# The first group's gates in a hybrid decoder step: raw products copied into the convolution's input tile

## The chip, the cores and the metric

The kernel runs as one program on one core of a Trainium2 chip. Its time is device time in microseconds (us) for one execution; lower is better. The core has five engines, each with an instruction queue of its own that is worked off in order: PE (TensorE, matrix products), DVE (VectorE), ACT (ScalarE), POOL (GpSimd) and SP (SyncE, which here only issues transfers).

## The reference

One layer of a decoder trunk is run for a prompt of 2048 tokens and for eight sample sequences of 4 tokens each, in float32. Cut to what matters here:

```python
h = rms_norm(x, w_norm1) * (1 + sc1) + sh1
proj = h @ w_in                    # all heads' q, k, v, gates from one projection
qkv, conv_new = short_conv(dn_qkv, conv_buf, w_conv)      # width 4, then silu
...                                # DeltaNet: per 64-token chunk in the reference
tmat = lower + eye(C)
sol = triangular_solve(tmat, rhs, lower=True, unit_diagonal=True)
...
o_dn  = rms(o_dn)  * w_dn_norm  * silu(dn_z)              # gated_head_norm
o_gla = rms(o_gla) * w_gla_norm * silu(gr)
x = x + gt1 * (concat(o_dn, o_gla) @ w_o)
...                                # then an MLP with squared ReLU, and a last norm
```

There are four DeltaNet heads and four GLA heads of 128 columns each. The gates that this change touches are `silu(dn_z)` and `silu(gr)`: eight projections of 128 columns, each followed by `z / (1 + exp(-z))`.

## The kernel before

The tokens are worked in four groups. Group 0 holds the 32 sample tokens and the first 512 of the prompt (544 columns, as two blocks of 272); groups 1 to 3 hold 512 prompt tokens each, one block. Activations lie transposed, 128 features on the partitions and tokens along the free axis. A product of float32 numbers is made of three products of rounded parts (`prod`, lines 243 to 245), so one projection of 128 columns is 8 x 3 matmuls per block, 48 in group 0. It goes into one of two PSUM banks named `gps`.

In group 0 every weight block is loaded once (line 221, on SP's queue), split into a high part (ACT, line 225) and a low part (DVE, line 226), and both are stored to DRAM (line 201); later groups load the two parts (line 217). The tiles `wb` have six buffers, and one block is prepared ahead.

Within a group the source goes: the four key projections, the four query projections, the four DeltaNet gates, the four value projections, and then for each GLA head its key, query and gate. A key, query or value projection ends in `conv`: ACT copies the product from PSUM into `craw` (one buffer, lines 824 to 827), DVE makes the width-4 convolution from it (lines 834 and 836), and a sigmoid follows. A `gate` reads its product twice on ACT, for the exponential (line 458) and, in group 0 alone, for a plain copy (line 462); the sigmoid follows (lines 153 to 155), DVE multiplies (line 464), and SP stores the result to `zscr` (line 465). In groups 1 to 3 DVE multiplies straight from PSUM.

Behind the first query projection the source calls `dn_inverse`, for the unit triangular matrices of the DeltaNet. DVE solves 32 x 32 blocks by 30 steps of two instructions (lines 912 and 914); the result goes to DRAM and back, head by head, into cleared tiles `Tm` (lines 921 and 923); a vector transpose (line 927) and small matmuls with copies between them (lines 933 to 953) put the blocks together. For each of the four heads it asks for three tiles of the name `t2`: one `Tm` and two `yt`. The name `t2` has three buffers. The result `Um` is first read in `dn_chain` (line 1015), which runs over the tokens in order and stands behind the first GLA key projection in the source.

Who waits for whom is not written by hand. The tile framework takes the instructions, in the order of the source as priority, and fixes an order for each engine; a tile that finds no free buffer of its name waits until an earlier one is released. So an engine's order differs from the source's where something had to wait. `sp` is the pool of such tiles, two buffers to a name unless `bufs` says otherwise. `rb` is a small tile in `dn_decay` (lines 797 to 799): four times, for group 0 alone, DVE writes it and a matmul reads it.

Of the kernel before, what the change touches and what calls it, by code (L numbers as in the profile page):

```python
# [8 lines left out]
F32 = mybir.dt.float32  # L9
# [7 lines left out]
P = 128  # L17
# [59 lines left out]
def tile_trunk(ctx: ExitStack, tc: tile.TileContext, a: dict):  # L77
# [8 lines left out]
    def gps():  # L86
        return pp.tile([P, 512], F32, name="gps", bufs=2)

    def mps():
        return pp.tile([P, 512], F32, name="mps", bufs=3)  # L90
# [7 lines left out]
    sp = stage.enter_context(tc.tile_pool(name="sp", bufs=2))  # L98
# [22 lines left out]
    def c32(k):  # L121
        o, n = NC32[k]
        return cf[:, o:o + n]
# [27 lines left out]
    def sigm(x):  # L151

        V.tensor_scalar(out=x, in0=x, scalar1=1e18, scalar2=None, op0=MIN)
        S.activation(out=x, in_=x, func=AF.Ln, bias=1.0)
        S.activation(out=x, in_=x, func=AF.Exp, scale=-1.0)
# [75 lines left out]
    def split(name, idx, nk=8, raw=None):  # L231
        hi, lo = ahead.pop((name, idx), None) or parts(name, idx, raw)
        if plan and plan[0] == (name, idx):
            plan.pop(0)
            if plan:
                ahead[plan[0]] = parts(*plan[0])
        return hi.rearrange("p (k c) -> p k c", k=nk), lo.rearrange("p (k c) -> p k c", k=nk)

    def prod(ps, w, x, ks, xs):

        n = len(ks)
        for i, (kw, kx) in enumerate(zip(ks, xs)):
            T.matmul(ps, lhsT=w[0][:, kw], rhs=x[0](kx), start=(i == 0), stop=False)  # L243
            T.matmul(ps, lhsT=w[0][:, kw], rhs=x[1](kx), start=False, stop=False)  # L244
            T.matmul(ps, lhsT=w[1][:, kw], rhs=x[0](kx), start=False, stop=(i == n - 1))  # L245

    def proj(g, blk, h):

        w = split("w_in", blk)
        out = []  # L250
        for c0, c1 in BLK[g]:
            ps = gps()
            prod(ps[:, 0:c1 - c0], w, (lambda k: h[0][:, k, c0:c1], lambda k: h[1][:, k, c0:c1]), range(8), range(8))
            out.append((ps[:, 0:c1 - c0], c0, c1))
        return out
# [197 lines left out]

    def gate(g, ct, h, blk):

        for ps, c0, c1 in proj(g, blk, h):
            e = sp.tile([P, 512], F32, name="e", bufs=3)[:, 0:c1 - c0]
            S.activation(out=e, in_=ps, func=AF.Exp, scale=-1.0)
            z = ps
            if g == 0:  # L460
                z = sp.tile([P, 512], F32, name="t2", bufs=3)[:, 0:c1 - c0]
                S.copy(out=z, in_=ps)
            sigm(e)
            V.tensor_tensor(out=e, in0=z, in1=e, op=MUL)
            Y.dma_start(out=zscr[ct, :, GC[g] + c0:GC[g] + c1], in_=e)
# [272 lines left out]
    def dn_decay(g, d, sm, sms):  # L738
# [34 lines left out]
        if g == 0:  # L773
            gs = sp.tile([32, 4], F32, name="gs", bufs=1)
            bs = sp.tile([32, 4], F32, name="bs", bufs=1)
            dn_gates(sms.unsqueeze(1), 32, 1, gs.unsqueeze(2), bs.unsqueeze(2))
            ps = mps()
            T.matmul(ps[0:32, 0:4], lhsT=c32("tri_s")[0:32], rhs=gs, start=True, stop=True)
            T.matmul(ps[0:32, 8:12], lhsT=c32("same_s")[0:32], rhs=gs, start=True, stop=True)
            gb = sp.tile([32, 4, 8], F32, name="gbs", bufs=1)  # L780
            V.tensor_tensor(out=gb, in0=gs.unsqueeze(2).broadcast_to([32, 4, 8]),
                            in1=c32("seq_s")[0:32].unsqueeze(1).broadcast_to([32, 4, 8]), op=MUL)
            pl = mps()
            T.matmul(pl[:, 0:32], lhsT=ones[0:32], rhs=gb.rearrange("p h b -> p (h b)"), start=True, stop=True)
            eLs = sp.tile([P, 4, 8], F32, name="eLs", bufs=1)
            S.activation(out=eLs, in_=pl[:, 0:32].rearrange("p (h b) -> p h b", h=4), func=AF.Exp)
            Gs = sp.tile([32, 4], F32, name="Gs", bufs=1)
            eGs = sp.tile([32, 4], F32, name="eGs", bufs=1)
            kcs = sp.tile([32, 4], F32, name="kcs", bufs=1)
            V.tensor_copy(out=Gs, in_=ps[0:32, 0:4])  # L790
            S.activation(out=eGs, in_=Gs, func=AF.Exp)
            V.tensor_tensor(out=kcs, in0=ps[0:32, 8:12], in1=Gs, op=SUB)
            S.activation(out=kcs, in_=kcs, func=AF.Exp)

            pb = mps()
            for hd in range(4):
                rb = sp.tile([P, P], F32, name="rb")
                V.tensor_scalar(out=rb[0:32], in0=ones[0:32], scalar1=gs[:, hd:hd + 1], scalar2=None, op0=MUL)
                T.matmul(pb[:, hd * 32:hd * 32 + 32], lhsT=rb[0:32], rhs=c32("tri_s")[0:32], start=True, stop=True)
            eGb = sp.tile([P, 4, 32], F32, name="eGbs", bufs=1)  # L800
            S.activation(out=eGb, in_=pb[:, 0:128].rearrange("p (h t) -> p h t", h=4), func=AF.Exp)
            Da = sp.tile([32, 4, 32], F32, name="Das", bufs=1)
            Db = sp.tile([32, 4, 32], F32, name="Dbs", bufs=1)
            for hd in range(4):
                for dst, mk in ((Da, "mas"), (Db, "mbs")):
                    V.scalar_tensor_tensor(out=dst[:, hd], in0=pb[0:32, hd * 32:hd * 32 + 32], scalar=Gs[:, hd:hd + 1],
                                           in1=c32(mk)[0:32], op0=SUB, op1=ADD)
            S.activation(out=Da, in_=Da, func=AF.Exp)
            S.activation(out=Db, in_=Db, func=AF.Exp, scale=-1.0)
            d.update(bs=bs, eGs=eGs, kcs=kcs, eLs=eLs, eGb=eGb, Da=Da, Db=Db)  # L810
            d["qv"] = sp.tile([P, 4, 3, 32], F32, name="qvs", bufs=1)
# [4 lines left out]
    def conv(g, ct, blocks, dst):  # L816

        off, tg = OFF[g], TG[g]
        raw = sp.tile([P, 515], F32, name="craw", bufs=1)
        xs = None  # L820
        for ps, c0, c1 in blocks:
            if c0 < off:
                xs = sp.tile([P, 8, 7], F32, name="xs")
                S.copy(out=xs[:, :, 3:7], in_=ps[:, 0:32].rearrange("p (b t) -> p b t", t=4))
                S.copy(out=raw[:, 3:3 + c1 - off], in_=ps[:, off:c1])  # L825
            else:
                S.copy(out=raw[:, 3 + c0 - off:3 + c1 - off], in_=ps)
        if g == 0:
            V.memset(raw[:, 0:3], 0.0)
        else:  # L830
            V.tensor_copy(out=raw[:, 0:3], in_=halo[0][:, ct, :])
        V.tensor_copy(out=halo[1][:, ct, :], in_=raw[:, 512:515])
        cp = dst[:, off:tg]
        V.tensor_scalar(out=cp, in0=raw[:, 0:512], scalar1=wconv[:, ct, 0:1], scalar2=None, op0=MUL)
        for i in range(1, 4):
            V.scalar_tensor_tensor(out=cp, in0=raw[:, i:i + 512], scalar=wconv[:, ct, i:i + 1], in1=cp, op0=MUL, op1=ADD)  # L836
        if g == 0:
            V.tensor_copy(out=xs[:, :, 0:3], in_=cst[:, ct])
            V.tensor_copy(out=cso[:, ct], in_=xs[:, :, 4:7])
            c4 = dst[:, 0:32].rearrange("p (b t) -> p b t", t=4)  # L840
            V.tensor_scalar(out=c4, in0=xs[:, :, 0:4], scalar1=wconv[:, ct, 0:1], scalar2=None, op0=MUL)
            for i in range(1, 4):
                V.scalar_tensor_tensor(out=c4, in0=xs[:, :, i:i + 4], scalar=wconv[:, ct, i:i + 1], in1=c4, op0=MUL, op1=ADD)
        e = sp.tile([P, 544], F32, name="ce", bufs=1)
        S.activation(out=e[:, 0:tg], in_=dst[:, 0:tg], func=AF.Exp, scale=-1.0)
        sigm(e[:, 0:tg])
        V.tensor_tensor(out=dst[:, 0:tg], in0=dst[:, 0:tg], in1=e[:, 0:tg], op=MUL)
# [19 lines left out]
    def dn_kproj(g, hd, h, d):  # L867
        conv(g, 4 + hd, proj(g, 12 + (hd // 2) * 8 + hd % 2, h), d["kT"][:, hd])
# [86 lines left out]
    def dn_qproj(g, hd, h, d):  # L955
        d["qT", hd] = sp.tile([P, 544], F32, name="cv")
        conv(g, hd, proj(g, 12 + (hd // 2) * 8 + 2 + hd % 2, h), d["qT", hd])
# [25 lines left out]
    def dn_vproj(g, hd, h, d):  # L983
        d["vT", hd] = sp.tile([P, 544], F32, name="cv")
        conv(g, 8 + hd, proj(g, 12 + (hd // 2) * 8 + 4 + hd % 2, h), d["vT", hd])
# [145 lines left out]
    def group(g):  # L1131
# [18 lines left out]
        def decays():  # L1150
            dn_decay(g, d, ts[0][1], ts[0][3])
# [46 lines left out]
        for hd in range(4):  # L1198
            step(lambda: gate(g, hd, h, 12 + (hd // 2) * 8 + 6 + hd % 2))
# [31 lines left out]
    sp = ctx.enter_context(tc.tile_pool(name="sp2", bufs=2))  # L1231
# [215 lines left out]
```

## Time and profile before

| what | value |
|---|---|
| time, median of 3 runs | 2951.27 us (2944.88 to 2957.69) |
| the profiled execution | 2961.44 us, span of the profile 2959.6 us |
| PE busy | 2835.0 us, 96% of the span |
| PE weight loads busy | 2400.3 us, 81% |
| DVE busy | 1494.0 us, 50% |
| ACT busy | 889.6 us, 30% |
| POOL busy | 265.9 us, 9% |
| mean granted clock of PE | 0.979 of full |

The span runs from the first to the last instruction of the profile; the profiled execution took 1.8 us more than its span and is one execution, which lies 10.2 us above the median of the three timed ones. Matmuls are pipelined, so a busy PE is not a PE at its peak. Idle time of an engine counts only where another engine waits for it.

### The profile page before, as it was taken

To read this page: it belongs to the slowest core of one execution; us is meant where nothing else is said; L and a number is where in the kernel's file an instruction comes from. 1 tells how busy PE (TensorE), PEld (TensorE's weight loads), DVE (VectorE), ACT (ScalarE), POOL (GpSimd) and SP (SyncE) were. 2 spreads that over 40 slices of the span, in tenths; PEclk is the share of its full clock that TensorE was granted. 3 is DMA by queue.
4 is the path that set the end of the run, shared out by engine and by line. 5 is a ranking of instruction groups with operands and counts; after the bars stand their busy time and mean duration, and the time that the engine had idled before them with its cause. 6 is when DMAs were issued, how large, how long until landed. Compare 5 with 4: busy or idle time off the path is not lost.

```text
span 2959.6 us, 43982 instructions
## 1 busy us (share of the span) xinstructions
PE 2835.0 (96%) x17311; PEld 2400.3 (81%) x17311; DVE 1494.0 (50%) x3564; ACT 889.6 (30%) x2238; POOL 265.9 (9%) x204
## 2 busy tenths in 40 slices
PE   7949999999999999989999999999899999999997
PEld 5849987887778777778899999999778888888886
DVE  5957778766767677547333333333744222222225
ACT  3625544344434344324122211222222100011102
POOL 0100000000000000041211212112210000000000
PEclk9969999999999999999999999999999999999999
DMA  7525644456536554586433333334774222222224
GB/s 274 193 73 197 230 149 156 141 168 243 196 124 216 178 175 147 197 281 235 152 144 128 143 136 131 146 129 148 273 259 160 100 99 87 100 93 92 100 88 154
DMA packets 174271, 476.08 MB, mean 161 GB/s; under 512 B 36960, under 2 KB 50656, under 8 KB 173296
## 3 DMA queue, kind: packets, MB, share of 16 engines
q1 hardware_dynamic: 167520, 451.88, 44.0%
q0 software_dynamic: 6544, 21.38, 2.3%
q8 instruction: 137, 2.24, 0.3%
q14 instruction: 70, 0.57, 0.1%
HBM read 331.68 MB, written 141.79 MB: 160 GB/s over the span
## 4 chain that ended last, share of the span: by engine, by line
PE 80%; DVE 8%; DMA 5%; issue 3%; ACT 2%; SPq 1%; POOL 1%; DVEq 0%; POOLq 0%; ACTq 0%
PE gps L244 12%; PE gps L245 12%; PE gps L243 12%; PE cps L244 10%; PE cps L245 10%; PE cps L243 10%; PE gps L419 1%; PE mps L419 1%; DMA wb<-w_in 1%; DMA zo<-zscr 1%; PE mps L1019 1%; DVE cv L836 1%; DVE Um L914 1%; PE mps L629 1%; DVE tb L912 1%
## 5 line engine op out<-in xcount | busy, mean ns | idle before, releaser
L243 PE MATMUL gps<-hb,wb 128*128 128x512 f32 (+1 forms) x1752 | 631.8, 361 | 5.0 <-ACT craw L825 3.0
L245 PE MATMUL gps<-hb,wb 128*128 128x512 f32 (+1 forms) x1752 | 625.7, 357 | 1.8 <-DMA wb<-k_w_o 1.6
L244 PE MATMUL gps<-hb,wb 128*128 128x512 f32 (+1 forms) x1752 | 627.2, 358 | 0.0
L243 PEld LDWEIGHTS gps<-hb,wb 128*128 128x128 f32 x1752 | 333.1, 190 | 57.5 <-issue 7.1
L244 PEld LDWEIGHTS gps<-hb,wb 128*128 128x128 f32 x1752 | 332.9, 190 | 44.4 <-issue 2.7
L245 PEld LDWEIGHTS gps<-hb,wb 128*128 128x128 f32 x1752 | 332.5, 190 | 44.5 <-DMA wb<-k_w_o 2.5
L245 PE MATMUL cps<-hb,wb 128*128 128x512 f32 (+1 forms) x968 | 343.9, 355 | 5.4 <-POOL wb L226 5.4
L243 PE MATMUL cps<-hb,wb 128*128 128x512 f32 (+1 forms) x968 | 343.4, 355 | 5.0 <-DVE gas L1247 3.7
L244 PE MATMUL cps<-hb,wb 128*128 128x512 f32 (+1 forms) x968 | 343.9, 355 | 0.0
L226 POOL TENSOR_TENSOR wb<-wb 128x1024 fp32r<-128x1024 f32 x72 | 172.4, 2394 | 746.4 <-PE gps L244 412.7
L243 PEld LDWEIGHTS cps<-hb,wb 128*128 128x128 f32 x968 | 183.7, 190 | 32.5 <-issue 4.1
L245 PEld LDWEIGHTS cps<-hb,wb 128*128 128x128 f32 x968 | 183.8, 190 | 32.0 <-POOL wb L226 6.1
L244 PEld LDWEIGHTS cps<-hb,wb 128*128 128x128 f32 x968 | 183.6, 190 | 26.5 <-issue 0.2
L225 ACT CAST wb<-wb 128x1024 fp32r<-128x1024 f32 (+1 forms) x104 | 109.2, 1050 | 307.5 <-DMA wb<-w_up 160.5
L1295 ACT ACTIVATE e<-cps 128x512 f32<-128x512 f32 (+1 forms) x96 | 50.0, 520 | 498.2 <-PE cps L245 498.1
L1298 DVE CAST a<-e 128x272 fp32r<-128x272 f32 (+1 forms) x96 | 58.7, 613 | 251.8 <-ACT e L1296 251.8
L1298 DVE CAST x<-e 128x512 fp32r<-128x512 f32 x64 | 27.3, 427 | 277.6 <-ACT e L1296 277.6
L243 PE MATMUL cps<-a,wb 128*128 128x272 f32 (+1 forms) x460 | 149.8, 326 | 5.8 <-DVE gas L1247 4.4
L244 PE MATMUL cps<-a,wb 128*128 128x272 f32 (+1 forms) x460 | 149.4, 325 | 0.0
L245 PE MATMUL cps<-a,wb 128*128 128x272 f32 (+1 forms) x460 | 149.0, 324 | 0.0
L1295 ACT ACTIVATE e<-gps 128x512 f32<-128x512 f32 (+1 forms) x64 | 32.8, 513 | 341.2 <-PE gps L245 340.1
L1243 DVE SCALAR_TENSOR_TENSOR a<-cps,modT,a 128x512 f32<-128x512 f32 (+1 forms) x81 | 58.1, 718 | 134.2 <-PE cps L245 134.2
(472 smaller groups left out, 5213.4 us busy)
## 6 DMA issues: line engine op xcount, KB each, us to landing
wb<-k_w_in SPq DMA_DIRECT2D x168, 512.0 KB, 4.3
wb<-k_w_up SPq DMA_DIRECT2D x80, 512.0 KB, 4.2
wb<-k_w_down SPq DMA_DIRECT2D x80, 512.0 KB, 4.2
k_w_up<-wb SPq DMA_DIRECT2D x64, 512.0 KB, 2.8
k_w_down<-wb SPq DMA_DIRECT2D x64, 512.0 KB, 2.8
k_w_in<-wb SPq DMA_DIRECT2D x56, 512.0 KB, 3.1
wb<-k_w_o SPq DMA_DIRECT2D x48, 512.0 KB, 4.5
wb<-w_up SPq DMA_DIRECT2D x32, 512.0 KB, 3.7
```

What stands on the lines that cost most here:

```text
L225: S.copy(out=hi, in_=raw[:, 0:n])
L226: (V if name in ("w_in", "w_ts0", "w_ts1") else G).tensor_tensor(out=lo, in0=raw[:, 0:n], in1=hi.bitcast(F32), op=SUB)
L243: T.matmul(ps, lhsT=w[0][:, kw], rhs=x[0](kx), start=(i == 0), stop=False)
L244: T.matmul(ps, lhsT=w[0][:, kw], rhs=x[1](kx), start=False, stop=False)
L245: T.matmul(ps, lhsT=w[1][:, kw], rhs=x[0](kx), start=False, stop=(i == n - 1))
L419: T.matmul(ps, lhsT=h[hh][:, 4 * q + kk, c0:c0 + P], rhs=w[:, kk, :], start=(kk == 0 and i == 0), stop=(kk == 3 and i == 2))
L629: T.matmul(pa[0:i0, n, i0:i0 + 32], lhsT=ko[:, n, o:o + I, :], rhs=Q3[:, n, i0:i0 + 32], start=True, stop=True)
L836: V.scalar_tensor_tensor(out=cp, in0=raw[:, i:i + 512], scalar=wconv[:, ct, i:i + 1], in1=cp, op0=MUL, op1=ADD)
L912: V.tensor_tensor(out=t, in0=Lb[:, j + 1:32, j:j + 1].broadcast_to([64, 31 - j, j]), in1=Tb[:, j:j + 1, 0:j].broadcast_to([64, 31 - j, j]) ...
L1243: V.scalar_tensor_tensor(out=out[:, lo:c1], in0=ps[:, lo - c0:c1 - c0], scalar=modT[:, gv, 0:1], in1=x[:, lo:c1], op0=MUL, op1=ADD)
L1295: S.activation(out=r, in_=ps, func=AF.Relu)
L1298: V.tensor_copy(out=hi, in_=r)
```

## The change

In group 0 the gate's plain copy of the product goes into a part of a `craw` tile, one tile for both blocks, and no longer into a `t2` tile for each block. The convolution asks for `craw` with 544 columns, so that both uses have one size; it still works with 515 of them. `craw` keeps one buffer. `rb` goes from two buffers to one, which frees 512 bytes on each partition; the larger `craw` takes 116 of them.

```diff
@@ gate
+        zs = sp.tile([P, 544], F32, name="craw", bufs=1) if g == 0 else None
         for ps, c0, c1 in proj(g, blk, h):
             e = sp.tile([P, 512], F32, name="e", bufs=3)[:, 0:c1 - c0]
             S.activation(out=e, in_=ps, func=AF.Exp, scale=-1.0)
             z = ps
             if g == 0:
-                z = sp.tile([P, 512], F32, name="t2", bufs=3)[:, 0:c1 - c0]
+                z = zs[:, c0:c1]
                 S.copy(out=z, in_=ps)
             sigm(e)
             V.tensor_tensor(out=e, in0=z, in1=e, op=MUL)
@@ dn_decay
-                rb = sp.tile([P, P], F32, name="rb")
+                rb = sp.tile([P, P], F32, name="rb", bufs=1)
@@ conv
-        raw = sp.tile([P, 515], F32, name="craw", bufs=1)
+        raw = sp.tile([P, 544], F32, name="craw", bufs=1)
```

## Rows read from the trace of the kernel before

**Rows 1.** The page: span, and busy tenths of 40 slices of 74 us.

```profile
span 2959.6 us, 43982 instructions
...
PE   7949999999999999989999999999899999999997
...
PEclk9969999999999999999999999999999999999999
```

**Rows 2.** Busy time by stretch: from, to, length; busy us (instructions); clock, DMA.

```profile
100.00:150.00 50.00, 45.66 (x352) 42.89 (x351) 50.00 (x152) 34.69 (x105) 6.27 (x5) 1.00 0.55 182
...
150.00:206.80 56.80, 17.57 (x275) 14.10 (x273) 29.87 (x88) 9.99 (x34) 0.00 (x0) 0.55 0.19 56
206.80:262.80 56.00, 52.37 (x397) 51.52 (x397) 37.62 (x96) 29.89 (x72) 0.00 (x0) 0.96 0.65 218
500.30:576.40 76.10, 75.65 (x603) 60.47 (x603) 61.90 (x172) 32.41 (x85) 0.00 (x0) 1.00 0.51 168
```

**Rows 3.** PE's waits, 148 to 210 us: total, times, longest.

```profile
PE cps L933 <- DVE Um L927: 24.7, 4, 17.9
```

**Rows 4.** Timeline of ACT: start, length, engine, line, operation [idle before].

```profile
144.65 0.40 ACT L458 ACTIVATE e<-gps 128x272 f32<-128x272 f32 x1 [1.07 <-PE gps L245]
...
148.68 0.38 ACT L458 ACTIVATE e<-gps 128x272 f32<-128x272 f32 x1
...
153.33 0.43 ACT L155 ACTIVATE e<-e 128x272 f32<-128x272 f32 x1
...
205.58 0.38 ACT L462 COPY t<-gps 128x272 f32<-128x272 f32 x1
```

**Rows 5.** Timeline of DVE: the last convolution step of query 3.

```profile
143.35 0.74 DVE L836 SCALAR_TENSOR_TENSOR cv<-craw,w_conv,cv 128x512 f32<-128x512 f32 x1
```

**Rows 6.** Lines 908, 953, 1015 by source: min/median/max ns, first to last start; groups 0, 1.

```profile
L908 DVE COPY Um<-vt x1: 676/676/676, 138.3 to 138.3; 64x1024 f32<-64x1024 f32 x1
...
L953 DVE COPY Um<-cps x4: 416/417/417, 183.1 to 206.9; 64x256 f32<-64x256 f32 x4
...
L1015 PE MATMUL cps<-vt,Um x8: 271/275/275, 262.8 to 267.1; 128*128 128x128 f32 x8
...
L908 DVE COPY Um<-vt x1: 682/682/682, 500.3 to 500.3; 64x1024 f32<-64x1024 f32 x1
...
L953 DVE COPY Um<-cps x4: 415/416/416, 542.1 to 574.5; 64x256 f32<-64x256 f32 x4
...
L1015 PE MATMUL cps<-rr,Um x28: 270/275/322, 576.5 to 599.7; 128*128 128x128 f32 x28
```

**Rows 7.** Tile `gps`, 140 to 240 us: the projection's first matmul, ns.

```profile
L243 PE MATMUL gps<-hb,wb x96: 283/288/593, 141.4 to 239.1; 128*128 128x272 f32 x96
```

**Rows 8.** Line 221 by source, 95 to 150 and 205 to 270 us.

```profile
L221 SPq DMA_DIRECT2D wb<-w_in x6: 383/394/476, 98.6 to 142.6; - x6
...
L221 SPq DMA_DIRECT2D wb<-w_in x8: 333/378/514, 214.9 to 263.0; - x8
```

**Rows 9.** Timelines of ACT and DVE: gates 0 and 1.

```profile
151.21 0.29 DVE L153 TENSOR_SCALAR e<-e 128x272 f32<-128x272 f32 x1
...
212.19 0.38 ACT L462 COPY t<-gps 128x272 f32<-128x272 f32 x1
...
217.17 0.44 DVE L464 TENSOR_TENSOR e<-t,e 128x272 f32<-128x272 f32 x1 [0.96 <-ACT e L155]
```

**Rows 10.** Timeline around 80 us: the matmuls and writes of `rb`.

```profile
80.52 0.63 PE L799 MATMUL mps<-cf,rb 32*128 32x32 f32 x4 [0.50 <-ACT eLs L786]
...
84.19 0.47 DVE L798 TENSOR_SCALAR rb<-cf,gs 32x128 f32<-32x128 f32 x2
```

**Rows 11.** SP's own waits, 140 to 270 us: total, times, longest.

```profile
SPq L923 <- DVE t L921: 18.1, 3, 6.0
...
SPq L916 <- DVE Um L914: 9.2, 1, 9.2
```

## Prediction

> **What bounds the kernel now.** I read the views from coarse to fine. The page's slices come first [rows 1]: TensorE (PE) is busy nine tenths or more in almost every slice of 74 us, and its granted clock is full everywhere but in two of the first four. The largest hole is the third slice (148 to 222 us), where PE is four tenths busy at a clock of 0.6 (part of the slice lies at the lower of the clock's two levels). So this is a PE-bound kernel with one gap worth looking at, and the change touches the code that runs there: the first group's gates.
>
> The table by stretch [rows 2] puts numbers on the gap. From 150.0 to 206.8 us PE works 17.57 of 56.80 us, at a granted clock of 0.55, so 39.2 us are idle and what is done is done near half rate. In the 56.0 us behind it PE works 52.37 us. The vector engine (DVE) works 29.87 us in the first stretch and 37.62 us in the second. Just ahead of the gap (100 to 150 us) DVE is busy 50.00 of 50.00 us and PE 45.66: in the first group DVE is the limit whenever both have work.
>
> Why does PE stand still? The list of its waits names the inverse [rows 3]: 24.7 us until the vector transpose of line 927. But that says only what PE did next, not what it could have done. The timeline of ScalarE (ACT) says that [rows 4]. Gate 0's two exponentials read PSUM at 144.65 and 148.68 us, and its sigmoids are finished at about 153.8. Its two copies into `t2` (line 462), which are all that still holds the two `gps` banks, come at 205.58 us and later, right behind the inverse's last use of that name: the twelve `t2` tiles of the inverse (four heads, three each) are asked for earlier in the source than the gates' and get the three buffers first. With both `gps` banks held no further projection can start, so gates 1 to 3 and the four value projections wait for an inverse which they do not need. Before that, nothing was missing for gate 1.
>
> **The change part by part.** *Destination of the copies.* Line 462 stays as it is in work: two copies per gate, 0.38 us each [rows 4]; only the address differs. Nothing is added on ACT. The new name `craw` has one buffer, last read by the convolution of query 3 at 143.35 us for 0.74 us [rows 5]. That is before gate 0's first exponential, so gate 0's copies can run directly behind their exponentials, at about 145 and 149 us instead of 205.6 and later, and the `gps` banks come free some 57 us earlier.
>
> *What PE gets to do in the gap.* Between 149 us and the chain's first use of the inverse (line 1015, at 262.8 us [rows 6]) lie seven products (gates 1 to 3, values 0 to 3), the inverse's own small matmuls and the transposes. I sum the work of both engines over 150.0 to 262.8 us (112.8 us long) and ask how short it can get.
> DVE: 29.87 + 37.62 = 67.5 us.
> PE: 17.57 us at a clock of 0.55 is about 9.7 us at full clock (an estimate: all of it scaled), plus 52.37, gives 62.0 us. That the clock matters is seen in the projection's matmuls: 288 ns in the median, 593 ns for the slowest, which came right after the gap [rows 7].
> The loads of weights: line 221 issues one block each 6.9 us behind the gap (eight from 214.9 to 263.0) and each 8.8 us ahead of it (six from 98.6 to 142.6) [rows 8]; seven of them are 48 to 62 us. None of the two others exceeds DVE, so DVE sets the stretch.
>
> If DVE were busy all the time, as from 100 to 150 us, the stretch would take 67.5 us: a gain of 45.3. The other end is the same stage in the second group, whose gates use no `t2` at all: 500.3 to 576.4 us, DVE busy 61.90 of 76.10, that is 0.81 [rows 2]. At 0.81 the stretch takes 83.0 us: a gain of 29.8. The new stretch resembles both. It has the first group's splitting of weights and its 544 columns, as the first; it also has the inverse's serial tail, four heads of transposes, small matmuls and transfers in which DVE alone does little, as the second. So I take half way, 0.907: 74.4 us, a gain of **38.4 us**. PE then is busy 62.0 of 74.4 us. Its own floor gives the extreme: 112.8 - 62.0 = 50.8 us.
>
> A check by another way: from the inverse's first copy (line 908) to the chain's first matmul it is 138.3 to 262.8 = 124.5 us in the first group and 76.2 us in the second [rows 6]. Were the first to come down to the second, 48 us would be won; the first has the more vector work, so less.
>
> On this sum the Trainium skill has a rule, in "Perfetto Trace Analysis", section "Identifying Performance Opportunities": improve the most-contended engine, and where regimes with different such engines follow each other, interleave them. In 100 to 150 us the trace agrees on which engine that is (DVE, 50.00 of 50.00). By occupancy alone the rule would give the 45.3 us; the second group's 0.81 says that a stage with this inverse does not reach it.
>
> *One buffer in place of three.* Gate n+1's copies must now wait for gate n's last multiply (line 464), and value 0's convolution for gate 3's. Behind the gap a gate holds its copies from 212.19 (first copy) to 217.61 us (end of the last multiply), 5.4 us [rows 9], against 6.3 us for one product (48 matmuls, 52.37 us for 397 of them [rows 2]) and 6.9 us between weights. So the buffer is free about when the next copy wants it, and there are two `gps` banks, which give 3 us more. Under a loaded DVE it is longer: gate 0's first exponential ended at 145.05 us and DVE took it up at 151.21 [rows 9]. I price this at 0 to 3 us for each of four hand-overs, 0 to 12 us, which lies inside the span between 1.00 and 0.81. What is queued behind a late copy on ACT is the next gate's exponential and the inverse's copies of lines 936 and 949, and for these PE waits.
>
> *`rb` with one buffer.* Four small vector operations in the decay of the samples now alternate with their matmuls. Before, the second pair was written 3.7 us after the first matmuls ran (80.52 to 84.19 us) [rows 10]. Two more such trips are 7.4 us at most, nothing at least. The result is read by the samples' masks, which are wanted only in the sample tasks behind the chain, and PE has the key projections meanwhile: I take 0. If that cover were gone, PE would wait those 7.4 us.
>
> *`craw` of 544 columns* in the convolution changes no instruction. Gates 4 to 7 of the first group copy to `craw` too when no convolution is left there; each lies between other products, so 0. The `zscr` stores of the gates (line 465), two per gate, are the same, but issued some 57 us earlier on SP's queue, among the inverse's transfers.
>
> Sum: span 2959.6 - 38.4 = 2921.2 us; the profiled execution took 2961.4, so 2923.0 for its like. That execution lies 10.2 us above the median of the runs, 2951.3; from the median I get **2912.9 us**. The work behind 262.8 us moves up unchanged.
>
> **The rivals.**
> *A new wait on SP's queue.* A gate's `e` tile is free only when its store has left, and there are three `e` buffers. SP is in order; in the gap it waited 9.2 us for the end of the elimination (line 916) and 18.1 us for cleared `t2` tiles (line 923) [rows 11]. If stores and weight loads get stuck behind these, up to 27.3 us are given back: a gain of 11.1, 2940 us. For it: the waits are there, and weights share that queue. Against it: the second group has the same queue and stage and its PE is busy 75.65 of 76.10 us [rows 2]. The one buffer of `craw` at its worst belongs here too (12 us: gain 26). The Trainium skill says in the same section of "Perfetto Trace Analysis" that a repeated gap on the engine that should be saturated can mean too few buffers; the gap of before agrees with it, and by this rule one buffer could bring such a gap back, smaller.
> *The gates stay behind.* If the copies keep their place on ACT behind line 949's of the last head, nothing moves: 2951 us. Against it: the exponentials of the same tiles already run 57 us earlier on that engine.
> *More than forecast.* PE fills the chain's wait with GLA projections and reaches its own floor: gain 45 to 51, 2900 to 2906 us.
> *Slower.* Vector work of gates and values gets ahead of the inverse's on DVE and the chain waits for `Um` at line 1015. The inverse ended at 207.3 us (line 953's last copy); all 37.62 us of vector work from behind the gap put ahead of it bring it to 244.9, still 18 us ahead of the old start of the chain. It turns the sign only if the inverse is late by over 55.5 us, and the time passes +0.5% at 70: 2966 us. In the second group it took 74.6 us (500.3 to 574.9) against 69.0 in the first [rows 6], so 5.6 us is the size to expect.
>
> **How the numbers follow.** Forecast (gain 30 to 45) 0.70, more 0.08, the queue or the buffer (gain 11 to 26) 0.13, no effect 0.06, slower 0.03. About 0.5%, 14.8 us, is what a measurement here can tell from no change. Half of the queue's case falls short of that, with no effect: 0.12 within, 0.03 slower, 0.85 faster. Range: the runs spread 6.4 us to either side of the median. Low end: 2951.3 - 45.3 - 6.4 = 2899.6, taken down to 2897 for the floor of PE. High end: the 29.8 gain and 6.4 give 2928; up to 2936 takes in about half of the queue's case. Left out is about 0.15.
>
> **What would show it.** Right: gate 0's copies at 145 to 150 us; PE over nine tenths busy or nearly so from 150 us on and at full clock in the third slice; the 24.7 us before line 933 nearly gone; the chain's first matmul between 217 and 233 us; the later stages the same length. Wrong: copies still behind the inverse (no effect); PE waiting for `craw` copies by many times 3 us (the buffer); SP in lines 916 or 923 while line 221's next load is due (the queue); line 1015 waiting for `Um` for tens of us (the inverse late).

## The result and the profile after

The changed kernel takes 2915.2 us (median of 4 runs, 2908.67 to 2918.18) against 2954.34 us before (4 runs), 39.1 us less; the ratio is 0.9867 with a 95% interval of 0.985 to 0.9883. The forecast was 38.4 us less and 2912.9 us, counted from a median before of 2951.3; the fourth run before has moved that median up by 3.1 us.

The page of the changed kernel, the slices that answer to [rows 1]:

```profile
span 2914.5 us, 43962 instructions
...
PE   7999999999999999999999999999899999999997
...
PEclk9999999999999999999999999999999999999999
```

The four of the third slice has become a nine, and so has the six of its clock. The table by stretch puts numbers to it (columns as in [rows 2]):

```profile
100.00:150.00 50.00, 47.12 (x364) 44.34 (x363) 50.00 (x148) 34.27 (x106) 6.45 (x5) 1.00 0.59 190
...
150.00:206.80 56.80, 53.47 (x500) 50.19 (x498) 53.80 (x159) 35.08 (x97) 0.00 (x0) 1.00 0.63 213
...
150.00:224.80 74.80, 69.84 (x709) 64.39 (x706) 69.78 (x199) 42.92 (x112) 0.00 (x0) 1.00 0.64 208
```

From 150 to 206.8 us PE starts 500 matmuls where it started 275, at a clock of 1.00 in place of 0.55, and stands idle for 3.3 us in place of 39.2. DVE does 53.80 us of work in place of 29.87. ACT's timeline shows why (lines 459 and 463 are the old 458 and 462; what stands below has moved by one line too):

```profile
146.81 0.40 ACT L459 ACTIVATE e<-gps 128x272 f32<-128x272 f32 x1 [1.07 <-PE gps L245]
147.10 0.38 ACT L463 COPY craw<-gps 128x272 f32<-128x272 f32 x1
...
151.21 0.37 ACT L463 COPY craw<-gps 128x272 f32<-128x272 f32 x1
...
157.71 0.38 ACT L463 COPY craw<-gps 128x272 f32<-128x272 f32 x1
```

Each copy follows its exponential; gate 1's come at 157.7 us, while the inverse is still in its elimination. PE's waits from 148 to 226 us (total, times, longest) have 0.3 us left of the 24.7 us of [rows 3]:

```profile
PE gps L243 <- ACT craw L826: 1.9, 1, 1.9
...
PE gps L243 <- ACT craw L463: 0.9, 1, 0.9
PE cps L934 <- DVE Um L928: 0.3, 1, 0.3
```

The inverse and the chain by source line answer to [rows 6]:

```profile
L909 DVE COPY Um<-vt x1: 676/676/676, 140.6 to 140.6; 64x1024 f32<-64x1024 f32 x1
...
L954 DVE COPY Um<-cps x4: 415/416/417, 194.9 to 224.9; 64x256 f32<-64x256 f32 x4
...
L1016 PE MATMUL cps<-vt,Um x8: 275/275/377, 224.8 to 227.0; 128*128 128x128 f32 x8
```

The chain starts at 224.8 us in place of 262.8, 38.0 us earlier. The span shrank by 45.1 us. Of the 7.1 us between, a part was won ahead of the chain as well: until the chain starts, PE has begun 283 of the products' first matmuls (line 243 into `gps`, from the span's start) and had begun 272 before. Eleven more, each with its two followers, are 33 matmuls of 0.132 us, 4.4 us of work that is no longer to be done behind it. The other 2.7 us are of the size by which runs differ: from the chain's start to the end it is 2689.7 us in this profile, 2680.9 when the changed kernel was run again, and 2678.0 in experiment 3, all with 283 begun; and 2696.8 before against 2692.4 and 2690.4 in experiments 1 and 4, all with 272. The granted clock goes with it: from 320 to 440 us it is 0.91 in this profile and 0.99 both in the repeat and in experiment 3, and PE starts 758 matmuls there against 794 and 795.

### The profile page after: what moved, and what is told of

It reads as the page before. It is cut to its first block, busy times and chain, and to the rows that moved or that the text cites. A ratio compares the mean times of both kernels' runs of the same rounds, so it can differ in the third digit from the quotient of the medians.

```text
span 2914.5 us, 43962 instructions
## 1 busy us (share of the span) xinstructions
PE 2830.3 (97%) x17311; PEld 2395.6 (82%) x17311; DVE 1488.0 (51%) x3564; ACT 889.3 (31%) x2238; POOL 265.6 (9%) x204
## 4 chain that ended last, share of the span: by engine, by line
PE 81%; DVE 8%; DMA 5%; issue 3%; ACT 2%; POOL 1%; SPq 0%; DVEq 0%; POOLq 0%; ACTq 0%
PE gps L244 12%; PE gps L245 12%; PE gps L243 12%; PE cps L244 10%; PE cps L245 10%; PE cps L243 10%; PE gps L419 1%; PE mps L419 1%; DMA wb<-w_in 1%; DVE cv L837 1%; PE mps L1020 1%; DMA xo<-oscr 1%; PE mps L630 1%; PE cps L164 1%; DVE Um L915 1%
```

## The experiments

The ratios are to the kernel before on the same chip, with 95% intervals. "Progress" in the table counts the first matmuls of products (line 243 into `gps`) that PE has started between 100 and 262.8 us: it says how far the projections have come. An edit is to the changed kernel where the text does not say "the kernel before".

| kernel | inverse starts | inverse ends | chain starts | progress | ratio |
|---|---|---|---|---|---|
| before | 138.3 | 207.3 | 262.8 | 219 | |
| changed | 140.6 | 225.3 | 224.8 | 268 | 0.9867 |
| 5: changed, again | 140.3 | 224.9 | 224.4 | 267 | 0.9863 |
| 1: gate 0 alone | 140.5 | 210.9 | 260.0 | 224 | 0.9986 |
| 2: no copy | 140.7 | 229.8 | 229.3 | 267 | 0.986 |
| 3: two buffers | 139.2 | 223.9 | 223.4 | 268 | 0.9845 |
| 4: `rb` alone | 137.7 | 206.5 | 259.8 | 221 | 0.9994 |
| 6: clears, first try | 144.7 | 229.4 | 228.9 | 273 | 0.9889 |
| 7: split on GpSimd | 152.1 | 257.0 | 261.8 | 220 | 1.0083 |
| 8: inverse later | 140.0 | 230.8 | 230.3 | 267 | 0.9869 |
| 9: vector work added | 139.3 | 232.4 | 231.9 | 251 | 0.9888 |
| 10: fewer taps | 140.1 | 229.0 | 228.5 | 268 | 0.9852 |

**1. Gate 0 alone.** Is it the line for `t2`, gate by gate?

```diff
-        zs = sp.tile([P, 544], F32, name="craw", bufs=1) if g == 0 else None
+        zs = sp.tile([P, 544], F32, name="craw", bufs=1) if g == 0 and ct == 0 else None
...
-                z = zs[:, c0:c1]
+                z = zs[:, c0:c1] if ct == 0 else sp.tile([P, 512], F32, name="t2", bufs=3)[:, 0:c1 - c0]
```

> Only gate 0's raw products go into the convolution's input tile; the seven other gates of the first group keep t2. My theory (the two PSUM banks are held by copies that stand behind the inverse in the line for t2): gate 0's banks come free at about 147 to 151 us, one more product (gate 1, 48 matmuls, some 6.3 us) runs, and then its two blocks hold the banks until the inverse has ended. Gain 5 to 10 us of the 39: ratio to before 0.9965 to 0.9985. Rival (it was the first gate's late start, or the order on the engines as a whole, that mattered): most of the gain comes with gate 0 alone, ratio 0.987 to 0.990.

Measured: 2952.81 against 2955.65 us, 0.9986 [0.9974, 0.9999], about 4 us (2.8 by the medians) where 5 to 10 were expected; the inverse also ends 3.6 us later than before. Its ACT timeline:

```profile
151.12 0.37 ACT L463 COPY craw<-gps 128x272 f32<-128x272 f32 x1
157.33 0.40 ACT L459 ACTIVATE e<-gps 128x272 f32<-128x272 f32 x1 [0.53 <-DVE hb L975]
158.96 0.40 ACT L459 ACTIVATE e<-gps 128x272 f32<-128x272 f32 x1 [0.86 <-PE gps L245]
209.22 0.38 ACT L463 COPY t<-gps 128x272 f32<-128x272 f32 x1
```

Gate 1's product runs and its exponentials come at 157.33 and 158.96 us, as in the changed kernel; then its copies wait for the inverse until 209.22 us. The block has moved on by exactly one gate. The rival (the first gate decides) falls.

**8. The same tiles, asked for in another order.** The kernel before, gates in `t2`, only the call of the inverse moved.

```diff
-                dn_inverse(d)
+                if g:
+                    dn_inverse(d)
...
+        if g == 0:
+            dn_inverse(d)
         step(ts_second, first_pre)
```

> The kernel before, gates still in t2, but in the first group the source calls the inverse behind the four DeltaNet gates. My theory (the three t2 buffers go to whoever asks first in the source): the gates' copies then run right behind their exponentials, from about 145 us, PE works through the gap, and the inverse, whose steps are free to start only with lower rank on DVE, ends later, the chain starts at 225 to 245 us: gain 20 to 40 us, ratio 0.987 to 0.993. Rival (not the order of asking but t2 itself is too small for both): copies and inverse block each other in turn, gain under 15 us, ratio over 0.995.

Measured: 2915.55 against 2953.15 us, 0.9869 [0.9847, 0.989]: the whole gain, with no tile renamed. Its ACT timeline:

```profile
146.10 0.38 ACT L462 COPY t<-gps 128x272 f32<-128x272 f32 x1
149.12 0.37 ACT L462 COPY t<-gps 128x272 f32<-128x272 f32 x1
```

So `t2` was not too small, and `craw` is nothing special: the three buffers went to the twelve requests that stood first in the source. The inverse's first copy still comes at 140.0 us; DVE takes it up between the gates' work.

**2. No copy at all.** Does the early release of PSUM matter?

```diff
-            if g == 0:
-                z = zs[:, c0:c1]
-                S.copy(out=z, in_=ps)
```

> The first group's gates make no copy at all: the multiply reads PSUM, as in the other groups. My theory (what cost was the wait for a t2 buffer, and a bank held until the multiply, some 5 us longer, is covered by the second bank and by the pace of the weights): the gain stays, ratio 0.985 to 0.990, line 464's wait moves on to PE for less than 5 us in all. Rival (the early release of PSUM is what the change brought): PE waits for the multiplies behind a loaded DVE, some 3 us for each of seven hand-overs, ratio 0.992 to 0.995.

Measured: 2913.17 against 2955.65 us, 0.986 [0.9839, 0.9881]. PE's waits from 140 to 300 us have the multiply (now line 461) once more, but short:

```profile
PE gps L243 <- DVE e L461: 1.8, 2, 1.6
```

A bank held until the multiply costs 1.8 us of waiting and nothing that the time shows. The chain starts at 229.3 us, 4.5 us later than in the changed kernel, with the same progress at 262.8 us; what delays it is open. The first group's copy is not needed; what cost was the tile that it waited for.

**3. Two buffers for the DeltaNet gates.**

```diff
-        zs = sp.tile([P, 544], F32, name="craw", bufs=1) if g == 0 else None
+        zs = sp.tile([P, 544], F32, name="ko" if ct in (0, 2) else "craw", bufs=1) if g == 0 else None
```

> As the changed kernel, but gates 0 and 2 copy into a tile of another name (that of the GLA mix, unused at that time), so the first group's DeltaNet gates have two buffers in turn. My theory (one buffer is free about when the next copy wants it; the trace of the changed kernel shows 0.9 us of waiting for such a copy): within 2 us of the changed kernel, ratio 0.986 to 0.988. Rival (one buffer in place of three costs up to 12 us): 3 to 10 us faster than the changed kernel, ratio 0.983 to 0.986.

Measured: 2909.54 us, 0.9845 [0.9825, 0.9865], lower than I expected and inside the rival's range. But the interval overlaps with that of the changed kernel, and the stretch doesn't speak for the rival: from the inverse's first copy to the chain it is 84.2 us in both, and the progress is 268 in both. PE still waits 1.0 us for such a copy. The clock differs too: over the ten runs of the changed kernel (the result and experiment 5) the time goes from 2925.89 us at a mean granted clock of 0.984 to 2906.51 us at 0.991, and three of the four runs here had 0.990 or 0.991. I take it for no difference that these runs can show.

**4. `rb` alone.** The kernel before with this one line of the change.

```diff
-                rb = sp.tile([P, P], F32, name="rb")
+                rb = sp.tile([P, P], F32, name="rb", bufs=1)
```

> The kernel before with rb at one buffer and nothing else. My theory: the four write-and-read pairs alternate beside the key projections, 0 to 2 us, ratio 0.999 to 1.001. Rival (the alternation stops PE, two more trips of 3.7 us): ratio 1.0015 to 1.0025, and the first copy of the inverse some 2 us or more later than at 138.3 us.

Measured: 0.9994 [0.9982, 1.0006]; the inverse starts at 137.7 us, not later. This line costs nothing. The inverse starts 2.3 us later in the changed kernel than before and 1.7 us later in experiment 8, which leaves `rb` alone; what delays it is not settled.

**5. The changed kernel again.**

> The changed kernel once more, beside the three others of this call on the same chip. Theory: ratio 0.985 to 0.988, some 38 us of it before the chain's first matmul. Rival (the span's 45 us were the truth): 0.984 or less.

Measured: 2912.31 against 2953.15 us, 0.9863 [0.9839, 0.9886]; the rival's 0.984 or less lies at the very edge of the interval.

**6 and 9. More vector work.** Does DVE set the stretch? The first try cleared a spare tile ahead of each gate.

```diff
+        if g == 0 and ct < 4:
+            scr = sp.tile([P, 544], F32, name="ko", bufs=1)
+            for _ in range(6):
+                V.memset(scr, 0.0)
```

> The changed kernel with 24 extra clears of a 544-column tile on DVE, six ahead of each of the first group's DeltaNet gates, about 0.5 us each, 12 us in all; nothing reads them. My theory (DVE sets the stretch from 150 us to the chain, it is busy 69.78 of 74.80 us there): 5 us fit into its gaps, 7 to 12 us come on top, the chain's first matmul at 231 to 237 us, ratio 0.989 to 0.991. Rival (PE sets it, busy 69.84 of 74.80 us, and fills a later chain with GLA products): 0 to 3 us, ratio 0.986 to 0.988, though the chain starts later.

It measured 2922.87 us, 0.9889 [0.9864, 0.9913], close to my theory's figure, and shows nothing of what it was made for. Line 459 of this kernel is the clear:

```profile
L459 DVE MEMSET ko<- x24: 512/512/512, 1.0 to 38.9; 128x544 f32 x24
```

Nothing made the clears wait, so they all ran in the first 39 us. The inverse starts at 144.7 us, and from there to the chain it is 84.2 us, as in the changed kernel. The second try ties them to the gate's exponential:

```diff
             S.activation(out=e, in_=ps, func=AF.Exp, scale=-1.0)
+            if g == 0 and ct < 4:
+                scr = sp.tile([P, 544], F32, name="ko", bufs=1)
+                V.tensor_copy(out=scr[:, 0:8], in_=e[:, 0:8])
+                for _ in range(3):
+                    V.memset(scr, 0.0)
```

> The changed kernel with extra vector work that can't run early: in each block of the first group's DeltaNet gates a copy of 8 columns of the exponential and three clears of a 544-column tile behind it, 24 clears of 0.51 us and 8 short copies, 13 to 14 us in all between 147 and about 175 us. My theory (DVE sets the stretch): the chain's first matmul comes 8 to 14 us later than at 224.4 to 224.8 us, at 232 to 239 us. If PE then has nothing else, ratio 0.989 to 0.991; if GLA products fill the time, the chain is late all the same but the ratio stays at 0.986 to 0.988. Rival (PE sets the stretch): the chain's first matmul within 5 us of the changed kernel's.

Measured: 2921.42 against 2954.14 us, 0.9888 [0.987, 0.9907]. The clears now run where they should, and the chain starts at 231.9 us, 7.1 to 7.5 us later (8.4 us counted from the inverse's first copy):

```profile
L464 DVE MEMSET ko<- x24: 512/512/512, 152.7 to 189.0; 128x544 f32 x24
```

PE's waits between 140 and 300 us:

```profile
PE gps L243 <- ACT craw L468: 8.9, 3, 4.2
```

The size is just short of what I expected, and the way of the harm is not the one that I had in mind: the clears stand ahead of the sigmoid's first step on DVE, the multiply comes later, `craw` is held longer, and PE waits 8.9 us for copies into it. So this is also the price of the single buffer when a gate's way through DVE is slow. The granted clock fell as well, to 0.94 from 150 to 231.9 us where the changed kernel's stretch has 1.00, so part of the loss may be the clock's.

**10. Less vector work.**

```diff
+        taps = 2 if g == 0 and ct >= 8 else 4
...
-        for i in range(1, 4):
+        for i in range(1, taps):
```

> The changed kernel with two of the four taps of the width-4 convolution left out in the first group's value projections, so that part of the output is not the reference's: eight vector instructions of 0.743 us fewer between 175 us and the chain, 5.9 us. My theory (DVE sets the stretch): the chain's first matmul 3 to 6 us earlier, at 218 to 222 us, ratio 0.984 to 0.987. Rival (PE, busy 69.84 of 74.80 us, or the inverse's own serial tail sets it): within 2 us of 224.4 to 224.8.

Measured: 2911.4 us, 0.9852 [0.9834, 0.987], not to be told from the changed kernel; the chain starts at 228.5 us, 4 us *later*. The first 70.5 us of the stretch:

```profile
150.00:220.50 70.50, 68.61 (x662) 64.49 (x660) 62.76 (x188) 42.19 (x110) 0.00 (x0) 1.00 0.71 242
```

In the same 70.50 us of the changed kernel DVE works 66.24 us and PE 65.54. DVE is down to 62.76 and PE is up to 68.61: PE was the limit as soon as DVE gave way. Progress at 262.8 us is the same 268. My theory that DVE sets the stretch falls in this direction; for the chain's start the rival's figure (within 2 us of 224.4 to 224.8) missed as well.

**7. The splitting of weights on GpSimd**, to take 12 us off DVE by another way.

```diff
-        (V if name in ("w_in", "w_ts0", "w_ts1") else G).tensor_tensor(...)
+        (V if name in ("w_ts0", "w_ts1") else G).tensor_tensor(...)
```

> The changed kernel with the low parts of the first group's input weights made on GpSimd (2.4 us each by the rows of the later weights) in place of DVE (1.2 us each); ten of them lie between 150 us and the chain, 12 us of vector work. My theory (DVE sets the stretch): PE's idle time there, 5.0 us, and 2.9 us from 100 to 150 us mostly go: 3 to 8 us faster than the changed kernel, ratio 0.983 to 0.986. Rival (PE sets it, or the splitting now takes 1.2 us longer on the way of each weight): no gain or a loss, ratio 0.986 to 0.991.

Measured: 2978.73 against 2953.15 us, 1.0083 [1.0063, 1.0102]: 66 us slower than the changed kernel beside it, far more than the rival's loss.

```profile
100.00:150.00 50.00, 37.04 (x244) 34.65 (x245) 44.19 (x105) 24.36 (x75) 15.23 (x9) 0.85 0.48 166
```

PE works only 37.04 of 50 us already ahead of the old gap. One split is 2397 ns in the median on GpSimd (the first 20 of them) against 1220 on DVE in the kernel before, and GpSimd's largest wait from 100 to 225 us is for products that free a `wb` buffer (total, times, longest):

```profile
POOL wb L226 <- PE gps L245: 71.8, 8, 13.8
```

A weight's split thus takes longer, on an engine that also makes `gm` for the decay matrices. The loss grows while there are such splits, the last of which starts at 372.9 us: against experiment 5 the first group's chain starts 37.4 us later and the second group's 62.4 us later (589.9 against 527.5 us), and the spans differ by 70.3 us. But PE's three largest waits from 100 to 262.8 us, 25.3 us in all, are for results of DVE, and none is named for a `wb`. How the splits' time and order on GpSimd reach PE is argued, not shown.

## Why the prediction held, step by step

**The cause** (copies that wait for `t2` behind the inverse hold both `gps` banks): right. Experiments 2 and 8 take the wait away in two other ways, without a copy and by the order of asking alone, and each gives the whole gain. Experiment 1 takes it away for one gate, and the block moves on by one gate for about 4 us.

**The place of the copies**: forecast at about 145 and 149 us, measured 147.10 and 151.21 us, the stage itself being 2.3 us later.

**The size**: right in sum (38.4 us forecast, 39.1 measured in the median; at the chain's start 38.0, and 4.4 of work done ahead), and the stretch from 150 us came out at 74.8 us where 74.4 was written. That it came so close is in part luck. The 74.4 was DVE's work over a share half way between 1.00 and the second group's 0.81. But in that stage of the second group PE is busy 75.65 of 76.10 us [rows 2], so the 0.81 tells that PE was full there, not how busy DVE can be beside the inverse. DVE's share came out at 0.933 in place of 0.907, its work at 69.78 us in place of 67.5, and the two misses nearly cancel.

PE's need was put at 62.0 us; PE did 69.84 us in the new stretch. Part of it is work that the sum did not have in this stretch: line 243 has 139 starts in it and had 128 from 150.0 to 262.8 us, so PE ran a piece of the GLA products ahead of the chain. That is 4.4 us of the 7.8; the other 3.4 I put down to the scaling of the old gap's busy time by the clock, which was an estimate. The trace bears out part of it: added up by line, the inverse's matmuls (old lines 933 to 952) took 18.5 us in the gap and take 12.2 now, which is 0.66 and not 0.55; on 17.57 us that makes 1.9 us. The last 1.5 us are not traced. GLA products ahead of the chain are the mechanism of the rival "more than forecast", though not its gain.

Both engines thus end at 0.93, and "DVE sets the stretch" was only half the truth: taking 5.9 us of vector work away wins nothing (10), adding 13 to 14 us costs some 7 (9). Nor is the chain's start the measure that I took it for: between 223.4 and 230.3 us (2, 3, 5, 8, 10) neither the progress nor the time follows it. At two of the three late starts PE has run other products meanwhile: at 228.5 us (10) and 230.3 us (8) it has begun 302 first matmuls in place of 283. At the third, 229.3 us (2), it has begun 285, so this does not explain all three.

**One buffer**: priced at 0 to 12 us, 0.9 us of waiting in the profile, no difference with two (3). The cover is not thick: 8.9 us of waiting came back when DVE had 0.5 us clears ahead of each sigmoid (9).

**`rb`**: taken as 0, measured 0.9994 with one inside its interval.

**SP's queue**: the waits moved. In the changed kernel, 140 to 240 us:

```profile
SPq L924 <- DVE cv L842: 7.3, 2, 6.4
...
SPq L917 <- DVE Um L915: 1.9, 1, 1.9
```

Line 917, the old 916, waits 1.9 us in place of 9.2 [rows 11], since stores and loads now fill the time ahead of it; PE shows no wait of its own for weights there, and with 5.0 us idle in the whole stretch it can have lost little by them.

**The inverse late**: 5.6 us were expected from the second group; it now takes 84.7 us in place of 69.0, so 15.7 us more. That term was too small by a factor of three. The sign did not turn, but the 55.5 us between the inverse's end and the chain, which the prediction took for room, are used up: in every kernel of the table that fills the gap, the chain's first matmul comes 0.5 us ahead of the end of the inverse's last copy, and in the changed kernel it stands on PE right behind the inverse's last matmuls (line 953 from 224.21 us, line 1016 from 224.81). So the chain's start now goes with the inverse's end.

On the rules of the Trainium skill. "Perfetto Trace Analysis", section "Identifying Performance Opportunities", which has one look for the most-contended engine and interleave regimes: the traces agree with the interleaving (the inverse's elimination now runs beside the gates, DVE 53.80 of 56.80 us); the gain by DVE's occupancy alone, 45.3 us, was not reached, since PE is as contended as DVE by then. Its sentence on repeated gaps and too few buffers holds for the gap of before only in part: it was one hole and no repeated gap, and experiment 8 fills it with the same number of buffers.

## What to carry to other kernels

A list of waits names what an engine did next, not what it could have done: ask which buffer keeps the next independent product from starting, and who stands ahead of it in the line for that name. Where buffers go out in the order of asking, a long serial stage that takes them all early blocks short users behind it; giving these another name, dropping their copy, or asking in another order were worth the same here, so take the one that costs no memory. When one stage ends at 0.93 on two engines, neither's busy time alone forecasts the next step, and an experiment that adds work must tie it to the place, or it will run somewhere else.

## What the runs showed that I had not expected

Taking 12 us of work off the busiest vector queue and putting it on an engine that was idle in that stretch (POOL 0.00 of 56.80 us) made the kernel 66 us slower. The work is on the way of each weight and takes twice as long there (2397 against 1220 ns); that this and the other queue's order make up the loss was not shown. And the same work behind the chain's start took 2678.0, 2680.9 and 2689.7 us in three profiles, whose mean granted clocks were 0.991, 0.990 and 0.987: a gain of this size is read better at the stage, where the two profiles of the changed kernel agree within 0.4 us (224.8 and 224.4), than from two spans, and beside the clock. To the microsecond the stage does not repeat either: experiment 4, whose time is that of the kernel before, starts the chain 3.0 us earlier.
